# Eleven groups of seven block products per MLP in place of seven, with two of each group's weight sums by accumulating DMA

## The chip, the core and the metric

The kernel runs on one NeuronCore of a Trainium2 chip, in one launch, with all operands in HBM at the start and the result in HBM at the end. The metric is the device time of that launch in microseconds (us), the median of several runs. A core has five engines that matter here, each with an instruction queue that it works off in order: TensorE (PE: matmuls and, beside them, weight loads), VectorE (DVE), ScalarE (ACT), GpSimd (POOL), and SyncE (SP), which here only starts DMA transfers. Engines wait for one another, and for transfers, on semaphores.

## What is computed

A decoder trunk of two layers on 256 tokens of width 2048, in float32: an RG-LRU block, an MLP, a dilated attention block, a second MLP, and a final RMSNorm. The change touches the two MLPs alone:

```python
def _mlp(h, w1, w2):
    u = jnp.einsum('bsd,df->bsf', h, w1)
    u = jnp.square(jax.nn.relu(u))
    return jnp.einsum('bsf,fd->bsd', u, w2)

x = x + _mlp(_rmsnorm(x, mlp_norm[i]), mlp_w1[i], mlp_w2[i])
```

Here `w1` is 2048 x 8192 and `w2` is 8192 x 2048.

## The kernel before

**Two-part numbers.** A float32 product is made of three matmuls. Each operand is cut into a high part (float32r) and a low rest: ScalarE copies the high part (line 108, `whi`), VectorE subtracts it from the original (line 112, `wlo`), and TensorE adds high x high, high x low and low x high in PSUM.

**Units.** Weights come in units of 128 x 2048 floats (1 MB). For each, SP starts a load, ScalarE makes the high cut, VectorE the low cut, and TensorE uses both. There are three `raw` buffers for loads, three for high cuts and three for low cuts. The functions `before_unit` and `behind_unit` write out the program's order: the load of unit i + 5 is issued ahead of unit i's matmuls, the low cut of unit i + 2 too, and the high cut of unit i + 3 just behind them. So a high cut waits until TensorE has left the unit three earlier. Callbacks (`after`) put the small work on results behind a unit or one unit later.

**An MLP in periods.** The hidden width of 8192 is handled in 8 periods of 1024. In period p TensorE multiplies the squared activations of that part by their rows of `w2`, and between those units it makes the activations of the next period, in 8 units called "w" (`plan_first`, 48 matmuls of 256 columns each; `u_done` and `u_low`, lines 487 to 501, square, cut and store them). The output has four chunks of 512 columns, kept in SBUF as `xc`. In the plain way (`plan_plain`) a chunk of a period takes two units of 24 matmuls of 512 columns, marked "s" in the order.

**Groups.** `plan_group` takes two chunks together and computes the 2 x 2 x 2 block products (two halves of the tokens, two halves of the period's rows, two chunks) with seven products in place of eight, in the manner of Winograd's form of Strassen's method. Each product has 12 matmuls of 512 columns and is a unit of its own with its own pair of cuts. Four of them use the loaded blocks b11, b21, b12, b22 (in `raw`, `q21`, `q12` and `q22`), and three use sums of them. Line 570 makes four sums of whole units on VectorE: qT = b11 - q12 ahead of t1 and qT + q22 ahead of t2 (the signs lie in how they are written), then q12 with q22 ahead of t3 and q21 with qT ahead of t4. The tiles `q21`, `q12`, `q22` and `qT` have one buffer each. The products add up in three PSUM banks, and `take` (line 574) adds these to `xc`.

On the other side sums of token blocks are needed: `sums_of_tokens` (lines 503 to 517) makes them with five VectorE instructions and one of ScalarE, once per quarter of a period's rows and for all groups of the period. It holds them back while a product of the running period still reads the last ones; `busy` says so and is cleared at product t3 ("s3").

**The order.** `ORDER` lists a period's units by hand: the seven products, 8 "w" and 4 "s", 19 in all. Periods 0 to 6 have a group, the last has only plain units and no "w".

Of the kernel before, what the change touches and what calls it, by code (L numbers as in the profile page):

```python
# [13 lines left out]
OP = mybir.AluOpType  # L14
# [13 lines left out]
NCH = D // 512  # L28
# [16 lines left out]
SOFT = (5, 3, 3, 3, 3)  # L45
LOOK_LO = 2
LOOK_HI = 3
GROUPS = range(7)
ORDER = ("b11", "w", "b21", "s", "w", "t1", "w", "t2", "b22", "w", "s", "w", "t3", "w", "s", "w", "t4", "w", "s")


@with_exitstack
def trunk(ctx: ExitStack, tc: tile.TileContext, a: dict, out: bass.AP):
    nc = tc.nc
# [10 lines left out]
    def unit(ap, width=UW):  # L65
        units.append({"ap": ap, "width": width})
        return len(units) - 1
# [74 lines left out]
    def item(u, fn):  # L142
        items.append((u, fn))
# [23 lines left out]
    def after(n, fn, *args):  # L167
        later.setdefault(now[0] + n, []).append((fn, args))
# [82 lines left out]
    def stand_w(ps, u, ks, w_at, first, last):  # L251
        hi, lo = split[u]
        for j, k in enumerate(ks):
            x = xT(k)
            s = slice((w_at + j) * 128, (w_at + j + 1) * 128)
            mm(ps, hi[:, s], x[:, 0:256], first and j == 0, False)
            mm(ps, hi[:, s], x[:, 256:512], False, False)
            mm(ps, lo[:, s], x[:, 0:256], False, last and j == len(ks) - 1)
# [12 lines left out]
    def acc_tile():  # L271
        return psum.tile([P, 512], F32, name="acc", bufs=4)
# [12 lines left out]
    def add_x(n, acc):  # L285
        for t in range(NT):
            nc.vector.tensor_add(xc[n][:, t, :], xc[n][:, t, :], acc[t])
# [19 lines left out]
    def new_aT(j):  # L307
        t = (perm if j < 16 else lru).tile([P, 512], F32R, name=f"aT{j}")
        state["aT", j] = t
        return t  # L310
# [176 lines left out]
    def u_done(p, j, ps):  # L487
        h, k = divmod(j, 4)
        if h == 0:
            squares[p, k] = lru.tile([P, 2, S], F32, name="uu", bufs=4)  # L490
        uu = squares[p, k][:, h, :]
        nc.vector.scalar_tensor_tensor(uu, ps[:, :S], 0.0, state["rstdB"], op0=OP.max, op1=OP.mult)
        nc.scalar.activation(uu, uu, AF.Square)
        t = new_aT(8 * (p % 2) + j)
        nc.scalar.activation(t[:, 0:256], uu, AF.Copy)
        after(1, u_low, t, uu)
        if h == 1 and p in GROUPS:
            after(1, waiting.append, (p, k))

    def u_low(t, uu):  # L500
# [29 lines left out]
    def plan_mlp(w1, w2, done):  # L530
        def plan_first(p, j):
            u = unit(w1[8 * p + j])

            def run():
                accs["u", p, j] = acc_tile() if p == 0 else psum.tile([P, 512], F32, name="g", bufs=2)
                stand_w(accs["u", p, j][:, :S], u, range(KD), 0, True, True)
                after(0, u_done, p, j, accs.pop(("u", p, j)))
            item(u, run)

        def plan_start():  # L540
            us = [unit(w1[j]) for j in (0, 4)]
            for at, ks in enumerate((range(0, 12), range(12, 16))):
                for u, j in zip(us, (0, 4)):
                    def run(u=u, j=j, ks=ks, at=at):
                        if at == 0:
                            accs["u", 0, j] = acc_tile()
                        stand_w(accs["u", 0, j][:, :S], u, ks, ks[0], at == 0, at == 1)
                        if at == 1:
                            after(1 if j == 0 else 0, u_done, 0, j, accs.pop(("u", 0, j)))
                    item(u, run)  # L550

        def plan_plain(p, n, h, last_part):
            u = unit(w2[((p // 2) * 4 + n) * 4 + (p % 2) * 2 + h])
            out_item(("m", n), u, aT, range(8 * (p % 2) + 4 * h, 8 * (p % 2) + 4 * h + 4), h == 0, h == 1,
                     done(n) if last_part else (lambda acc, n=n: add_x(n, acc)))

        def plan_group(p, n0):


            q, bank = {}, {}  # L560

            def fetch(name, h, n, tag):
                q[name] = (wts.tile([P, UW], F32, name="raw", bufs=RAW_BUFS) if tag == "raw"
                           else lru.tile([P, UW], F32, name=tag))
                nc.sync.dma_start(q[name], w2[((p // 2) * 4 + n0 + n) * 4 + (p % 2) * 2 + h])

            def add(to, a, b):
                if to not in q:
                    q[to] = lru.tile([P, UW], F32, name=to)
                nc.vector.tensor_add(q[to], q[a], q[b])  # L570

            def take(n, t, b, sign):
                x = xc[n0 + n][:, t, :]
                (nc.vector.tensor_add if sign > 0 else nc.vector.tensor_sub)(x, x, bank[b])

            def product(loads, sums, source, what, b, first, takes):
                def load_all():
                    for l in loads:
                        fetch(*l)

                def make_all():
                    for m in sums:
                        add(*m)
                u = form(load_all, make_all, lambda: q[source])

                def run():
                    if first:
                        bank[b] = acc_tile() if b != "A" else psum.tile([P, 512], F32, name="tr", bufs=2)
                    hi, lo = split[u]
                    get = standing(p, what)  # L590
                    for k in range(4):
                        xh, xl = get(k)
                        s = slice(k * 512, (k + 1) * 512)
                        mm(bank[b], xh, hi[:, s], first and k == 0, False)
                        mm(bank[b], xh, lo[:, s], False, False)
                        mm(bank[b], xl, hi[:, s], False, k == 3)
                    for t in takes:
                        after(0 if what == "a22" else 1, take, *t)
                    if what == "s3":
                        busy[0] = None  # L600
                    if what == "a11":
                        busy[0] = p
                item(u, run)

            return {
                "b11": lambda: product([("b11", 0, 0, "raw")], [], "b11", "a11", "A", True, [(0, 0, "A", 1)]),
                "b21": lambda: product([("q21", 1, 0, "q21")], [], "q21", "a12", "B", True, [(0, 0, "B", 1)]),
                "t1": lambda: product([("q12", 0, 1, "q12")], [("qT", "b11", "q12")], "qT", "s0", "C", True,
                                      [(1, 1, "C", -1)]),
                "t2": lambda: product([("q22", 1, 1, "q22")], [("qT", "qT", "q22")], "qT", "s1", "A", False,  # L610
                                      [(1, 0, "A", -1)]),
                "b22": lambda: product([], [], "q22", "s2", "C", False, [(1, 0, "C", -1)]),
                "t3": lambda: product([], [("q12", "q12", "q22")], "q12", "s3", "A", False, [(1, 1, "A", -1)]),
                "t4": lambda: product([], [("q21", "q21", "qT")], "q21", "a22", "A", False, [(0, 1, "A", 1)]),
            }

        plan_start()
        for j in (1, 5, 2, 6, 3, 7):
            plan_first(0, j)
        for p in range(8):  # L620
            if p == 7 and done is final_done:
                item(None, load_g)
            if p < 7:
                nxt = iter([(p + 1, j) for j in (0, 4, 1, 5, 2, 6, 3, 7)])
            plain = [(n, h) for n in range(2 if p in GROUPS else 0, NCH) for h in range(2)]
            g = plan_group(p, 0) if p in GROUPS else {}
            for what in (ORDER if p in GROUPS else ("s", "w") * 8):
                if what == "w":
                    if p < 7:
                        plan_first(*next(nxt))  # L630
                elif what != "s":
                    g[what]()
                elif p == 7 and plain[0][0] == NCH - 1 and done is final_done:
                    final_items([unit(w2[(12 + n) * 4 + 2 + h]) for n, h in plain])
                    break
                else:
                    plan_plain(p, *plain.pop(0), p == 7)
# [190 lines left out]
    for n in range(NCH):  # L828
        xg[n] = new_xg(n)
        rs = [wts.tile([P, UW], F32, name="raw", bufs=RAW_BUFS) for _ in range(3)] if n == 0 else rs  # L830
        for h in range(2 if n == 0 else 1):
            w = 2 if n == 0 else 4
            nc.sync.dma_start(xg[n][:, h * w:(h + 1) * w, :], a["xT"][:, 4 * n + h * w:4 * n + (h + 1) * w, :])
            for i in range(3):
                if n or i == 0:
                    s = slice(n * 512 + h * w * 128, n * 512 + (h + 1) * w * 128)
                elif h:
                    s = slice(0, 512)
# [5 lines left out]
        for h in range(2 if n == 0 else 1):  # L844
            w = 2 if n == 0 else 4
# [31 lines left out]
    for n in range(NCH):  # L877
        s = slice(n * 512, (n + 1) * 512)
# [127 lines left out]
```

## Time and profile before

| | us |
|---|---|
| median of 3 runs | 2173.51 (2171.34 to 2175.61) |
| the profiled execution | 2173.91 |
| its span, first to last instruction | 2172.1 |
| TensorE busy | 2144.1 |
| VectorE busy | 1600.6 |
| ScalarE busy | 1167.5 |
| one period of an MLP, from the first product of one to that of the next | 86.30 |

The span is what the profiler sees between the first and the last instruction; the time has 1.8 us around it. A view of the profile shows instructions with their start, their duration in us, the engine, the line, what is written and read, and in square brackets how long the engine had been idle before and which instruction ended that wait. Matmuls overlap one another, so the pace of TensorE is the distance from one start to the next and not a matmul's duration.

### The profile page before, as it was taken

How to read it: one execution, taken by the hardware profiler on the slowest of the kernel's cores; microseconds unless marked ns; L12 is line 12 of the kernel's file. 1: busy time of each engine (PE TensorE's matmuls, PEld its weight loads, DVE VectorE, ACT ScalarE, POOL GpSimd, SP SyncE). 2: the span in 40 equal slices, each digit the busy share in tenths (PEclk: the TensorE clock that was granted, in tenths of full speed). 3: DMA queues.
4: the chain of work that ended last, by engine and by line, in shares of the span. 5: the costliest groups of instructions: out<-in, count | busy, mean ns of one | idle time of the engine just before them, and what ended most of it. 6: DMA issues, size and time to landing. Idle time of an engine off the chain costs nothing.

```text
span 2172.1 us, 32089 instructions
## 1 busy us (share of the span) xinstructions
PE 2144.1 (99%) x13602; PEld 1940.1 (89%) x13602; DVE 1600.6 (74%) x1748; ACT 1167.5 (54%) x1261; POOL 78.9 (4%) x42
## 2 busy tenths in 40 slices
PE   7999999999999999999999999999999999999997
PEld 7999988999999999999888888889999999999996
DVE  8898954688887888787555555556888878878875
ACT  5777755554555554455545544456455455554543
POOL 2221100000000000000000000000000000000002
PEclk9999999999999999999999999999999999999999
DMA  6565555556455455554554454455554563645543
GB/s 231 204 208 194 197 199 185 183 197 230 148 221 213 156 216 192 194 213 175 176 193 158 171 175 174 157 191 190 198 214 166 204 231 137 232 178 194 210 176 134
DMA packets 61712, 413.56 MB, mean 190 GB/s; under 512 B 6784, under 2 KB 7168, under 8 KB 13440
## 3 DMA queue, kind: packets, MB, share of 16 engines
q1 hardware_dynamic: 61568, 411.51, 52.1%
q8 instruction: 106, 1.74, 0.3%
q14 instruction: 38, 0.31, 0.0%
HBM read 409.39 MB, written 2.10 MB: 189 GB/s over the span
## 4 chain that ended last, share of the span: by engine, by line
PE 83%; DVE 10%; ACT 4%; issue 1%; POOL 0%; DMA 0%; SPq 0%; DVEq 0%; ACTq 0%
PE acc L171 53%; PE g L171 24%; DVE wlo L112 6%; PE tr L171 4%; ACT whi L108 2%; DVE q L570 1%; ACT sT L187 1%; DVE sT L188 0%; PE tr L211 0%; DVE aT L501 0%; DVE sw L512 0%; PE tr L670 0%; PE g L678 0%; DVE xT L849 0%; DVE sw L514 0%
## 5 line engine op out<-in xcount | busy, mean ns | idle before, releaser
L108 ACT ACTIVATE whi<-raw 128x2048 fp32r<-128x2048 f32 (+2 forms) x348 | 646.8, 1860 | 562.2 <-PE acc L171 336.5
L112 DVE TENSOR_TENSOR wlo<-raw,whi 128x2048 fp32r<-128x2048 f32 (+2 forms) x348 | 779.9, 2245 | 214.9 <-ACT whi L108 214.7
L171 PE MATMUL g<-xT,whi 128*128 128x256 f32 x3616 | 642.4, 281 | 0.0
L171 PE MATMUL acc<-whi,aT 128*128 128x512 f32 x1840 | 580.5, 390 | 0.0
L171 PEld LDWEIGHTS g<-xT,whi 128*128 128x128 f32 x3616 | 559.1, 188 | 8.7
L171 PE MATMUL g<-xT,wlo 128*128 128x256 f32 x1808 | 508.5, 281 | 2.2 <-DVE wlo L112 2.2
L171 PEld LDWEIGHTS acc<-whi,aT 128*128 128x128 f32 x1840 | 345.4, 188 | 69.6
L171 PE MATMUL acc<-wlo,aT 128*128 128x512 f32 x920 | 358.3, 389 | 0.0
L171 PEld LDWEIGHTS g<-xT,wlo 128*128 128x128 f32 x1808 | 346.2, 191 | 4.6 <-DVE wlo L112 4.6
L171 PE MATMUL acc<-xT,whi 128*128 128x256 f32 x1760 | 309.7, 281 | 6.5 <-ACT whi L108 6.1
L171 PEld LDWEIGHTS acc<-xT,whi 128*128 128x128 f32 x1760 | 270.7, 191 | 7.5 <-ACT whi L108 6.3
L171 PE MATMUL acc<-xT,wlo 128*128 128x256 f32 x880 | 247.2, 281 | 8.3 <-DVE wlo L112 8.1
L171 PE MATMUL acc<-whi,xT 128*128 128x512 f32 x768 | 245.9, 396 | 0.0
L171 PEld LDWEIGHTS acc<-wlo,aT 128*128 128x128 f32 x920 | 172.8, 188 | 33.4
L108 ACT ACTIVATE whi<-q 128x2048 fp32r<-128x2048 f32 x56 | 107.2, 1914 | 176.4 <-DVE q L570 137.8
L171 PEld LDWEIGHTS acc<-xT,wlo 128*128 128x128 f32 x880 | 168.0, 191 | 9.6 <-DVE wlo L112 9.4
L171 PEld LDWEIGHTS acc<-whi,xT 128*128 128x128 f32 x768 | 144.3, 188 | 30.6
L171 PE MATMUL acc<-wlo,xT 128*128 128x512 f32 x384 | 150.4, 392 | 0.0
L112 DVE TENSOR_TENSOR wlo<-q,whi 128x2048 fp32r<-128x2048 f32 x56 | 128.2, 2289 | 19.2 <-ACT whi L108 19.2
L108 ACT ACTIVATE whi<-qT 128x2048 fp32r<-128x2048 f32 x28 | 53.7, 1918 | 132.8 <-DVE qT L570 132.8
L112 DVE TENSOR_TENSOR wlo<-qT,whi 128x2048 fp32r<-128x2048 f32 x28 | 64.2, 2292 | 47.9 <-ACT whi L108 47.9
L171 PEld LDWEIGHTS acc<-wlo,xT 128*128 128x128 f32 x384 | 72.2, 188 | 15.1
(175 smaller groups left out, 1940.3 us busy)
## 6 DMA issues: line engine op xcount, KB each, us to landing
raw<-in_w SPq DMA_DIRECT2D x214, 1024.0 KB, 4.8
raw<-in_w_qkv SPq DMA_DIRECT2D x48, 1024.0 KB, 4.8
q<-in_w SPq DMA_DIRECT2D x42, 1024.0 KB, 6.9
raw<-in_w_in SPq DMA_DIRECT2D x35, 1024.0 KB, 4.8
raw<-in_w_out SPq DMA_DIRECT2D x20, 1024.0 KB, 4.8
raw<-in_w_o SPq DMA_DIRECT2D x16, 1024.0 KB, 4.8
raw<-in_w_g SPq DMA_DIRECT2D x10, 512.0 KB, 3.4
raw<-in_w_in SPq DMA_DIRECT2D x11, 256.0 KB, 5.7
```

Of the source, the lines that this page charges most:

```text
L108: nc.scalar.activation(split[i][0][:, s], r, AF.Copy)
L112: nc.vector.tensor_sub(split[i][1][:, s], r, split[i][0][:, s].bitcast(F32))
L171: nc.tensor.matmul(o, l, r, start=start, stop=stop, skip_group_check=True)
L187: nc.scalar.activation(hi_out, src, AF.Copy)
L570: nc.vector.tensor_add(q[to], q[a], q[b])
```

## The change

`GROUPS` becomes a number of groups for each period, 2, 1, 2, 1, 2, 1, 2, 0, and `ORDER` has a list for each number. A period of two covers all four chunks by groups: 14 products and 8 "w", no plain unit. Its second group's b11 stands ahead of the first group's t4. Periods of one keep their order. The two sums ahead of t3 and t4 are no longer VectorE instructions. An accumulating DMA, started by GpSimd, adds q22 to q12 and qT to q21 in SBUF; both are issued where t2's sum is made. `busy` is cleared at t3 of a period's last group. All lines behind the table move down by 7 to 11.

```diff
-GROUPS = range(7)
-ORDER = ("b11", "w", "b21", "s", "w", "t1", "w", "t2", "b22", "w", "s", "w", "t3", "w", "s", "w", "t4", "w", "s")
+GROUPS = (2, 1, 2, 1, 2, 1, 2, 0)
+ORDER = {
+    0: ("s", "w") * 8,
+    1: ("b11 0", "w", "b21 0", "s", "w", "t1 0", "w", "t2 0", "b22 0", "w", "s", "w", "t3 0", "w", "s", "w", "t4 0", "w", "s"),
+    2: ("b11 0", "w", "b21 0", "t1 0", "w", "t2 0", "b22 0", "w", "t3 0", "b11 1", "t4 0", "w",
+        "b21 1", "t1 1", "w", "t2 1", "b22 1", "w", "t3 1", "w", "t4 1", "w"),
+}
...
-        if h == 1 and p in GROUPS:
+        if h == 1 and GROUPS[p]:
             after(1, waiting.append, (p, k))
...
             def add(to, a, b):
+                if to == a != "qT":
+                    nc.gpsimd.dma_start(q[to], q[b], accum_op=OP.add)
+                    return
...
-                    if what == "s3":
+                    if what == "s3" and last_group:
                         busy[0] = None
...
-                "t2": lambda: product([("q22", 1, 1, "q22")], [("qT", "qT", "q22")], "qT", "s1", "A", False,
+                "t2": lambda: product([("q22", 1, 1, "q22")], [("qT", "qT", "q22"), ("q12", "q12", "q22"),
+                                                  ("q21", "q21", "qT")], "qT", "s1", "A", False,
...
-                "t3": lambda: product([], [("q12", "q12", "q22")], "q12", "s3", "A", False, [(1, 1, "A", -1)]),
-                "t4": lambda: product([], [("q21", "q21", "qT")], "q21", "a22", "A", False, [(0, 1, "A", 1)]),
+                "t3": lambda: product([], [], "q12", "s3", "A", False, [(1, 1, "A", -1)]),
+                "t4": lambda: product([], [], "q21", "a22", "A", False, [(0, 1, "A", 1)]),
...
-            plain = [(n, h) for n in range(2 if p in GROUPS else 0, NCH) for h in range(2)]
+            plain = [(n, h) for n in range(2 * GROUPS[p], NCH) for h in range(2)]
```

The first place where the order differs is VectorE's queue, from the low cut of b21 to that of t2's sum, in a period with one group of before. A row is the line, the operation, and what it writes from what; numbers tell the buffers apart.

```order
L112 TENSOR_TENSOR wlo_6082<-q21_5960,whi_6067 128x2048
L112 TENSOR_TENSOR wlo_6101<-raw_5980,whi_6097 128x2048
L574 TENSOR_TENSOR xc0_68<-xc0_68,tr_6084 128x512
L492 SCALAR_TENSOR_TENSOR uu_6155<-g_6103,rstdB_4114 128x256
L112 TENSOR_TENSOR wlo_6162<-raw_6039,whi_6152 128x2048
L570 TENSOR_TENSOR qT_6177<-raw_5859,q12_6080 128x2048
L501 TENSOR_TENSOR aT8_6158<-uu_6155,aT8_6158 128x256
L112 TENSOR_TENSOR wlo_6182<-qT_6177,whi_6179 128x2048
L574 TENSOR_TENSOR xc0_68<-xc0_68,acc_6164 128x512
L112 TENSOR_TENSOR wlo_6215<-raw_6099,whi_6210 128x2048
L570 TENSOR_TENSOR qT_6177<-qT_6177,q22_6160 128x2048
```

Two other low cuts (a plain unit and a "w") stand between the cut of b21 and the sum for t1. Now VectorE's queue in a period of two of the changed kernel, from the first group's t4 (the cut of `q21_5967`) to the second group's t1 and t2.

```order
L119 TENSOR_TENSOR wlo_6367<-q21_5967,whi_6357 128x2048
L508 TENSOR_TENSOR aT9_6363<-uu_6360,aT9_6363 128x256
L119 TENSOR_TENSOR wlo_6386<-raw_6285,whi_6381 128x2048
L584 TENSOR_TENSOR xc1_69<-xc1_69,tr_6091 128x512
L119 TENSOR_TENSOR wlo_6406<-q21_6304,whi_6401 128x2048
L580 TENSOR_TENSOR qT_6420<-raw_6208,q12_6365 128x2048
L584 TENSOR_TENSOR xc2_70<-xc2_70,tr_6388 128x512
L584 TENSOR_TENSOR xc0_68<-xc0_68,tr_6091 128x512
L119 TENSOR_TENSOR wlo_6426<-qT_6420,whi_6422 128x2048
L499 SCALAR_TENSOR_TENSOR uu_6360<-g_6428,rstdB_4114 128x256
L119 TENSOR_TENSOR wlo_6485<-raw_6384,whi_6477 128x2048
L580 TENSOR_TENSOR qT_6420<-qT_6420,q22_6404 128x2048
```

The sum for t1 now stands directly behind the low cut of b21, and that cut (`q21_6304`) only two cuts behind the last one that reads the old contents of the same buffer.

The second place is the SP queue, with what each load waits for in brackets: here of before, from b11 of a period (`raw_5859`) to its q22.

```order
L565 DMA raw_5859<-in_w2_0 128x2048 [waits DMAHW4_49,DVE_49,Activation_49]
L87 DMA raw_5900<-in_w1_0 128x2048 [waits DMAHW5_49,DVE_49,Activation_49]
L565 DMA q21_5960<-in_w2_0 128x2048
L87 DMA raw_5980<-in_w2_0 128x2048 [waits DMAHW6_49,DVE_49]
L87 DMA raw_6039<-in_w1_0 128x2048 [waits DMAHW0_49,DVE_49]
L565 DMA q12_6080<-in_w2_0 128x2048
L87 DMA raw_6099<-in_w1_0 128x2048 [waits DMAHW2_49,DVE_49]
L565 DMA q22_6160<-in_w2_0 128x2048
```

And the changed kernel's loads of the second group of a period of two, from its b11 (`raw_6208`) to its q22; DMASW is an accumulating DMA.

```order
L572 DMA raw_6208<-in_w2_0 128x2048 [waits DMAHW7_49,DVE_49]
L94 DMA raw_6285<-in_w1_0 128x2048 [waits DMAHW3_49,DVE_49]
L572 DMA q21_6304<-in_w2_0 128x2048 [waits DMASW7_49,DVE_49]
L572 DMA q12_6365<-in_w2_0 128x2048 [waits DMAHW1_49,DMASW6_49]
L94 DMA raw_6384<-in_w1_0 128x2048 [waits DMAHW5_49,DMAHW2_49]
L572 DMA q22_6404<-in_w2_0 128x2048 [waits DMAHW4_49]
```

The load of the group's q21 had nothing to wait for before; it now waits for the accumulating DMA into that buffer and for VectorE, and the three loads behind it stand in line.

More of the change, by code (lines that the diff above doesn't have):

```diff
@@ L555, in plan_plain, with plan_group @@
                      done(n) if last_part else (lambda acc, n=n: add_x(n, acc)))
-        def plan_group(p, n0):
+        def plan_group(p, n0, last_group):
             q, bank = {}, {}
@@ L624, in plan_mlp @@
                 nxt = iter([(p + 1, j) for j in (0, 4, 1, 5, 2, 6, 3, 7)])
-            plain = [(n, h) for n in range(2 if p in GROUPS else 0, NCH) for h in range(2)]
-            g = plan_group(p, 0) if p in GROUPS else {}
-            for what in (ORDER if p in GROUPS else ("s", "w") * 8):
+            plain = [(n, h) for n in range(2 * GROUPS[p], NCH) for h in range(2)]
+            g = [plan_group(p, 2 * n, n == GROUPS[p] - 1) for n in range(GROUPS[p])]
+            for what in ORDER[GROUPS[p]]:
                 if what == "w":
@@ L631, in plan_mlp @@
                 elif what != "s":
-                    g[what]()
+                    g[int(what[-1])][what[:-2]]()
                 elif p == 7 and plain[0][0] == NCH - 1 and done is final_done:
```

## The prediction

> **What bounds the kernel now.** I read the page first, for the engines' shares.
>
> ```profile
> span 2172.1 us, 32089 instructions
> PE 2144.1 (99%) x13602; PEld 1940.1 (89%) x13602; DVE 1600.6 (74%) x1748; ACT 1167.5 (54%) x1261; POOL 78.9 (4%) x42
> ```
>
> TensorE is busy throughout, but a share over the whole span says nothing about one stage. So next come the windows of single periods in the first MLP, cut where a period's first product starts (columns: us, then PE, PEld, DVE, ACT, POOL busy, granted clock, DMA share, GB/s).
>
> ```profile
> 688.80:775.10 86.30, 86.12 (x566) 78.90 (x565) 70.77 (x72) 44.14 (x39) 0.00 (x0) 1.00 0.53 197
> 775.10:861.40 86.30, 86.12 (x566) 78.89 (x565) 70.50 (x71) 44.07 (x39) 0.00 (x0) 1.00 0.52 195
> ```
>
> Every period takes 86.30 us, TensorE fills it, and VectorE is busy for 70.6, which leaves it 15.7. The chain of waits in that window gives the price of each kind of unit on TensorE: a "w" (48 matmuls), a product (12), a plain half chunk (24).
>
> ```profile
> 705.48 5.65 PE g L171 x48
> 711.13 2.72 PE acc L171 x12
> 730.60 5.44 PE acc L171 x24
> ```
>
> 8 x 5.65 + 7 x 2.72 + 4 x 5.44 = 86.0: a period is TensorE's work without gaps, so fewer matmuls make it shorter only if the weights keep arriving. The last view is VectorE's timeline at a period's start, with TensorE's rows there.
>
> ```profile
> 774.61 1.37 DVE L287 TENSOR_TENSOR xc<-xc,acc 128x512 f32<-128x512 f32 x2 [0.31 <-PE acc L171]
> 775.89 0.29 DVE L511 TENSOR_TENSOR sw<-uu 128x128 f32<-128x128 f32 x1
> ...
> 777.75 0.69 DVE L188 TENSOR_TENSOR sT<-sw,sT 128x512 fp32r<-128x512 f32 x1 [0.72 <-ACT sT L187]
> 778.36 2.29 DVE L112 TENSOR_TENSOR wlo<-q,whi 128x2048 fp32r<-128x2048 f32 x1
> 780.57 2.28 DVE L112 TENSOR_TENSOR wlo<-raw,whi 128x2048 fp32r<-128x2048 f32 x1
> 782.77 0.68 DVE L574 TENSOR_TENSOR xc<-xc,tr 128x512 f32<-128x512 f32 x1
> 783.66 0.42 DVE L492 SCALAR_TENSOR_TENSOR uu<-g,rstdB 128x256 f32<-128x256 f32 x1 [0.21 <-PE g L171]
> 785.49 2.29 DVE L112 TENSOR_TENSOR wlo<-raw,whi 128x2048 fp32r<-128x2048 f32 x1 [1.41 <-ACT whi L108]
> 787.70 2.29 DVE L570 TENSOR_TENSOR qT<-raw,q 128x2048 f32<-128x2048 f32 x1
> 789.90 0.42 DVE L501 TENSOR_TENSOR aT<-uu,aT 128x256 fp32r<-128x256 f32 x1
> 792.03 2.29 DVE L112 TENSOR_TENSOR wlo<-qT,whi 128x2048 fp32r<-128x2048 f32 x1 [1.71 <-ACT whi L108]
> ```
>
> ```profile
> 775.09 0.39 PE L171 MATMUL tr<-whi,aT 128*128 128x512 f32 x1
> ...
> 783.46 0.39 PE L171 MATMUL acc<-whi,aT 128*128 128x512 f32 x1
> ...
> 797.27 0.39 PE L171 MATMUL acc<-whi,sT 128*128 128x512 f32 x1
> 797.50 0.39 PE L171 MATMUL acc<-wlo,sT 128*128 128x512 f32 x1
> ```
>
> Three prices follow. A full-width VectorE pass takes 2.29 us and the next starts 2.20 after it. A weight sum delays the low cut of its own result by 4.33 (787.70 to 792.03), since ScalarE's high cut lies between and VectorE waits for it in order. Before the first low cut of a period VectorE must finish the last token sum: it starts it 3.27 after the period (778.36 against 775.09). And there is slack: t1's low half is ready at 794.32, and TensorE asks for it at 797.50, so 3.2 us are left.
>
> **The change: matmuls.** Each of the 8 added groups replaces 4 x 5.44 by 7 x 2.72: -2.72 us, -21.8 in all. It holds only if TensorE never waits, and the period of two is where that is in doubt. I number its units from 0: b11 0, w 1, b21 2, t1 3, w 4, t2 5, b22 6, w 7, t3 8, b11' 9, t4 10, w 11, b21' 12, t1' 13, w 14, t2' 15, b22' 16, w 17, t3' 18, w 19, t4' 20, w 21; T is the time from its start at which TensorE could begin a unit. The high cut of unit u can begin only when unit u-3 has left TensorE (three buffers); it did so 0.08 us after a w ended:
>
> ```profile
> 783.54 1.92 ACT L108 ACTIVATE whi<-raw 128x2048 fp32r<-128x2048 f32 x1 [3.62 <-PE g L171]
> 785.37 0.40 ACT L493 ACTIVATE uu<-uu 128x256 f32<-128x256 f32 x1
> ```
>
> and the low cut followed at 785.49, 1.95 after the high one began.
>
> **VectorE's first half (T0 to T8).** With the plain unit gone between b21 and t1, in VectorE's order: low cut of b21 at 3.27, sum for t1 at 5.47, t1's low cut at 9.80, ready at 12.09. TensorE wants it at 11.09 + 0.23 = 11.32: wait 0.77. Then an update of xc (0.60) and uu (0.33; each its duration less the 0.09 by which passes overlap), unit 4's low cut, ready at 15.23 against 14.81: 0.42. The second sum starts at 15.14, t2's low cut at 19.47, ready at 21.76 against 20.88: 0.88. Units 6 and 7 the same way: 0.08 and 0.42. Sum 2.57; T8 moves from 30.55 to 33.12.
>
> **The load of b21' (T8 to T13).** The SP queue issues in order, and the q21 buffer is read by b21 and again by t4. Its two rows:
>
> ```profile
> 699.19 2.29 DVE L112 TENSOR_TENSOR wlo<-raw,whi 128x2048 fp32r<-128x2048 f32 x1 [1.38 <-ACT whi L108]
> ...
> 701.51 2.53 SPq L87 DMA_DIRECT2D raw<-in_w x2
> ```
>
> ```profile
> DMA to landing us min/median/max: 4.7/6.9/8.8
> ```
>
> A load waiting for a low cut issues 0.03 after it (701.51 against 701.48), and a load of q lands 4.7 us later at best. Unit 12's load now waits for unit 10's low cut, and unit 10's high cut for T8. In a row from T8: 0.08, high cut 1.95, low cut 2.29, issue 0.03, landing 4.7: 9.05. Then b21's high cut 1.95, its low cut 2.20, the sum for t1' behind it in VectorE's order and t1's cuts 4.33, low cut 2.29: 19.82. TensorE wants it at three products, a w, b21' and 0.23 after T8: 8.16 + 5.65 + 2.72 + 0.23 = 16.76. Wait 3.06. Queued behind that load on SP are q12', w 14 and q22'; they land by T8 + 18 at 2.9 us apiece (1 MB at about 360 GB/s, an estimate: 190 GB/s at a queue share of 52.1%), in time for their cuts.
>
> ```profile
> q1 hardware_dynamic: 61568, 411.51, 52.1%
> HBM read 409.39 MB, written 2.10 MB: 189 GB/s over the span
> ```
>
> I take the minimum, 4.7, as SP was blocked before and the queue is then empty; by the median, 6.9, the wait would be 5.3 and the sum below 8 x 2.2 = 18 more. [...]
>
> **The second half.** Counting from the start of t1's low cut, the second sum comes at 4.73, t2's low cut is ready at 11.35 against 10.66 (0.69), units 16 and 17 wait 0.08 and 0.42. The token sums at the end (2.47 each, 775.89 to 778.36) pile up in the last four units and delay the next period's w by 0.79; not where the last period follows, which has no token sums. Sum 1.98.
>
> **Two sums per group by DMA.** They free VectorE of 2 x 2.20, already left out above, and on Pool they queue before nothing (its busy time in the windows is 0.00); in periods of one TensorE did not wait before, so nothing comes of it there. The trace has no accumulating DMA. From below it takes 4.7, a load's best. From above 17.6: twice the slowest load, 8.8, as two tensors are read. The first can begin when t1's sum has read q12, at 7.76, the second when t2's sum ends, at 17.43; the second must land by t4's high cut at 33.20. It has 15.8 us, or 12.7 each if the two go one behind the other. I take values nearer the load: no cost. [...]
>
> **The sum.** Per period of two: -2.72 + 2.57 + 3.06 + 1.98 = +4.89; eight of them +39.1; less 0.79 in each of the two layers' last: +37.5. On the profiled execution's own 2173.9 (span 2172.1 and 1.8 around it; the runs' median is 2173.5) that is 2211 us.
>
> **Rivals.** *TensorE alone decides (0.10).* VectorE's work in a period of two is 70.6 + 3 more full passes (3 more cuts; 4 sums as before) x 2.20 + 3 more updates of xc x 0.60: 79.0 of 83.6 us; if the buffers smooth this and t1' does not wait, the time is 2173.9 - 21.8 = 2152. The place is t1' (unit 13), and it decides where all waits of a period of two stay under 2.72. Against it: the 9.05 to landing and the 4.33 are both in rows, and make 3.06 alone.
> *Only the load of b21' costs (0.12).* VectorE's lateness is all of 0.4 to 0.9 us pieces, which small errors could remove: 8 x (3.06 - 2.72) = +2.7, 2176.6.
> *The accumulates land late (0.13).* At 17.6 each in a row the second lands at 43.0, 9.8 late, and the load of b21' with it: 8 x 9.8 more, 2290; it decides above 12.7 each. [...]
>
> **The numbers.** My forecast has 0.65, at 2211. The low end takes in the second rival, 2176; the high end accumulates of 14.8 us each (2.1 over 12.7, twice, in eight periods: +34), 2245. Outside lie 0.10 below and some 0.05 above. About 0.2% (4.3 us) is what a measurement can tell from no change: faster 0.10, same 0.12, slower 0.78.
>
> **What would show it.** Right: windows of about 91 us for periods of two and 86.3 for the others; TensorE waiting some 3 us on the low cut of qT at the second group's t1, behind an SP queue that waits for the low cut of q21; the accumulates landing within 12 us. Wrong: 83.6 us for periods of two, or the high cut of q21 or q12 waiting for the software DMA.

## The result, and the profile after

The changed kernel takes 2224.03 us (median of 4 runs, 2223.12 to 2225.34), the kernel before 2172.66 on the same chip (4 runs, 2171.34 to 2175.61): a ratio of 1.0233, with a 95% interval of 1.0221 to 1.0246. The forecast was 2211. The direction held, and the loss was about 14 us larger than the sum. Two of the forecast's mechanisms are in the trace as it worked them out, but the costliest wait is one that it did not have, and this one hides the load's wait that it did have: that the sum came near is in part luck.

The page of the changed kernel, its busy times and the chain that ended last:

```profile
span 2223.5 us, 32196 instructions
...
PE 2144.4 (96%) x13506; PEld 1925.2 (87%) x13506; DVE 1641.8 (74%) x1784; ACT 1218.0 (55%) x1285; POOL 117.1 (5%) x86
...
PE 72%; DVE 15%; ACT 7%; issue 3%; DMA 2%; POOL 0%; SPq 0%; DVEq 0%; ACTq 0%
```

There are 96 matmuls fewer, yet TensorE is busy for as long, and idle for 4% of the span in place of 1%. VectorE holds 15% of the chain. Neither line says where; the windows of one period of two and the period of one behind it do (columns as in the prediction):

```profile
608.69:702.15 93.46, 87.01 (x554) 77.78 (x552) 77.05 (x76) 49.46 (x40) 3.44 (x4) 0.98 0.66 206
702.15:788.17 86.02, 86.02 (x566) 79.02 (x565) 68.12 (x70) 45.38 (x41) 1.72 (x2) 1.00 0.70 242
```

14 products and 8 "w" need 83.3 us (14 x 2.72 + 8 x 5.65) and took 93.46. The forecast was 91.2 (86.30 + 4.89). The period of one, 86.02, is 0.28 shorter than before, where the forecast had no change.

**The first half came as worked out.** VectorE's rows at the start of that period:

```profile
611.97 2.28 DVE L119 TENSOR_TENSOR wlo<-q,whi 128x2048 fp32r<-128x2048 f32 x1
614.17 2.28 DVE L580 TENSOR_TENSOR qT<-raw,q 128x2048 f32<-128x2048 f32 x1
618.50 2.29 DVE L119 TENSOR_TENSOR wlo<-qT,whi 128x2048 fp32r<-128x2048 f32 x1 [2.04 <-ACT whi L115]
...
623.84 2.28 DVE L580 TENSOR_TENSOR qT<-qT,q 128x2048 f32<-128x2048 f32 x1
...
628.16 2.29 DVE L119 TENSOR_TENSOR wlo<-qT,whi 128x2048 fp32r<-128x2048 f32 x1 [1.71 <-ACT whi L115]
```

From the period's start at 608.69 the forecast had the low cut of b21 at 3.27, the sums at 5.47 and 15.14 and the low cuts of qT at 9.80 and 19.47; the rows give 3.28, 5.48, 15.15, 9.81 and 19.47. TensorE's waits in the same period, in order:

```profile
620.84 0.50 PE L178 MATMUL acc<-wlo,sT 128*128 128x512 f32 x1 [0.67 <-DVE wlo L119]
630.51 0.50 PE L178 MATMUL tr<-wlo,sT 128*128 128x512 f32 x1 [0.61 <-DVE wlo L119]
634.00 0.47 PE L178 MATMUL acc<-whi,sT 128*128 128x512 f32 x1 [0.71 <-DVE xc L584]
...
647.71 0.39 PE L178 MATMUL tr<-whi,aT 128*128 128x512 f32 x1
650.40 0.76 PE L178 MATMUL tr<-whi,aT 128*128 128x512 f32 x1 [2.31 <-DVE xc L584]
650.96 0.63 PE L178 MATMUL tr<-wlo,aT 128*128 128x512 f32 x1
651.39 1.05 PE L178 MATMUL tr<-whi,aT 128*128 128x512 f32 x2
652.24 0.63 PE L178 MATMUL tr<-wlo,aT 128*128 128x512 f32 x1
...
675.11 0.47 PE L178 MATMUL acc<-whi,sT 128*128 128x512 f32 x1 [0.58 <-DVE xc L584]
...
693.66 0.47 PE L178 MATMUL tr<-whi,aT 128*128 128x512 f32 x1 [1.51 <-DVE xc L584]
```

The first two are the low halves of t1 and t2. Each costs the bracket and 0.16 to 0.18 more until the pace of 0.23 a matmul is back: 0.83 and 0.79, forecast 0.77 and 0.88. The third, b22, waits 0.87, and not for a cut: its releaser is line 584, a take. The fourth, at 650.40, is the costliest and in no term of the forecast: t4 starts 2.46 us late, again for a take. After it single matmuls stand 0.43 apart in place of 0.23; the granted clock from 650.40 to 653.50 is 0.50. The last two rows are b22 and t4 of the second group, 0.73 and 1.68 late, for takes again.

**What t4 waits for.** VectorE from t4's low cut on, and then the SP queue, from the load of b21':

```profile
644.53 2.29 DVE L119 TENSOR_TENSOR wlo<-q,whi 128x2048 fp32r<-128x2048 f32 x1 [1.41 <-ACT whi L115]
...
647.37 2.29 DVE L119 TENSOR_TENSOR wlo<-raw,whi 128x2048 fp32r<-128x2048 f32 x1 [0.21 <-ACT whi L115]
649.58 0.68 DVE L584 TENSOR_TENSOR xc<-xc,tr 128x512 f32<-128x512 f32 x1
653.67 2.29 DVE L119 TENSOR_TENSOR wlo<-q,whi 128x2048 fp32r<-128x2048 f32 x1 [3.42 <-ACT whi L115]
655.88 2.28 DVE L580 TENSOR_TENSOR qT<-raw,q 128x2048 f32<-128x2048 f32 x1
...
660.21 2.29 DVE L119 TENSOR_TENSOR wlo<-qT,whi 128x2048 fp32r<-128x2048 f32 x1 [0.85 <-ACT whi L115]
```

```profile
646.85 0.80 SPq L572 DMA_DIRECT2D q<-in_w  x2
```

The row at 649.58 is the take of t3. t3 and t4 add up in the same PSUM bank ("A" in the code), so t4 may begin only when VectorE has read t3's result out. The take is held back by one unit and stands behind the low cut of a "w" (647.37). With plain units and "w" between t3 and t4, as in a period of one, that costs nothing (TensorE is busy for all of the 86.02 above). In the period of two only b11' is between them.

Then the load of b21'. It was issued at 646.85, 0.03 after t4's low cut (644.53 + 2.29), as worked out. t4's high cut began at 642.58 (the profile's ScalarE row is below), 0.08 after T8 by the forecast's count, so t1's low cut should have been ready at 642.58 - 0.08 + 19.82 = 662.32; it was ready at 662.50.

```profile
642.58 1.92 ACT L115 ACTIVATE whi<-q 128x2048 fp32r<-128x2048 f32 x1 [3.62 <-PE g L178]
```

```profile
663.23 0.39 PE L178 MATMUL acc<-whi,sT 128*128 128x512 f32 x1
663.45 0.39 PE L178 MATMUL acc<-wlo,sT 128*128 128x512 f32 x1
```

But TensorE reached t1' only at 663.23, because t4 had held it up, and asked for the low half at 663.45. The 3.06 of the load was there and found nobody waiting.

**The accumulating DMAs came in time.** Their issues, from GpSimd, beside a plain load on SP (KB each, then median us to landing), and the landing of those that read qT, the second of each group:

```profile
raw<-in_w SPq DMA_DIRECT2D x190, 1024.0 KB, 5.1
...
q<-q POOLq DMA_DIRECT2D x22, 1024.0 KB, 11.6
q<-qT POOLq DMA_DIRECT2D x22, 1024.0 KB, 10.4
```

```profile
DMA to landing us min/median/max: 7.7/10.4/13.0
```

The DMA that reads qT starts last; even its slowest, 13.0, is within the 15.8 that the forecast gave it. All 44 together landed in 7.7 to 13.2 us. In the period shown 15.0 to 18.0 lie between the start of one's issue and the high cut that reads its result, and no high cut of the whole run waited for one.

### The profile page after: what moved, and what is told of

Its sections match the earlier page's. It is cut to its first block, busy times and chain, and to the rows that moved or that the text cites. A ratio compares the mean times of both kernels' runs of the same rounds, so it can differ in the third digit from the quotient of the medians.

```text
span 2223.5 us, 32196 instructions
## 1 busy us (share of the span) xinstructions
PE 2144.4 (96%) x13506; PEld 1925.2 (87%) x13506; DVE 1641.8 (74%) x1784; ACT 1218.0 (55%) x1285; POOL 117.1 (5%) x86
## 4 chain that ended last, share of the span: by engine, by line
PE 72%; DVE 15%; ACT 7%; issue 3%; DMA 2%; POOL 0%; SPq 0%; DVEq 0%; ACTq 0%
PE acc L178 46%; PE g L178 20%; DVE wlo L119 8%; ACT whi L115 6%; PE tr L178 4%; DVE qT L580 3%; DMA q<-in_w 2%; DVE xc L584 1%; DMA xg<-in_xT 0%; PE tr L218 0%; ACT sT L194 0%; PE tr L681 0%; PE g L689 0%; DMA raw<-in_w_in 0%; DVE xT L860 0%
## 5 line engine op out<-in xcount | busy, mean ns | idle before, releaser
L115 ACT ACTIVATE whi<-raw 128x2048 fp32r<-128x2048 f32 (+2 forms) x324 | 600.9, 1857 | 499.7 <-PE acc L178 328.9
L119 DVE TENSOR_TENSOR wlo<-raw,whi 128x2048 fp32r<-128x2048 f32 (+2 forms) x324 | 724.4, 2240 | 172.7 <-ACT whi L115 172.3
L178 PE MATMUL acc<-whi,aT 128*128 128x512 f32 x1392 | 440.3, 391 | 0.0
L178 PEld LDWEIGHTS acc<-whi,aT 128*128 128x128 f32 x1392 | 261.3, 188 | 52.7
L178 PE MATMUL acc<-wlo,aT 128*128 128x512 f32 x696 | 271.1, 390 | 0.0
L115 ACT ACTIVATE whi<-q 128x2048 fp32r<-128x2048 f32 x88 | 168.2, 1911 | 155.2 <-PE g L178 98.5
L119 DVE TENSOR_TENSOR wlo<-q,whi 128x2048 fp32r<-128x2048 f32 x88 | 201.4, 2289 | 62.6 <-ACT whi L115 62.6
L178 PEld LDWEIGHTS acc<-wlo,aT 128*128 128x128 f32 x696 | 130.7, 188 | 25.3
L119 DVE TENSOR_TENSOR wlo<-qT,whi 128x2048 fp32r<-128x2048 f32 x44 | 100.8, 2292 | 66.8 <-ACT whi L115 66.8
L178 PE MATMUL tr<-whi,aT 128*128 128x512 f32 x352 | 121.0, 405 | 27.5 <-DVE xc L584 27.5
## 6 DMA issues: line engine op xcount, KB each, us to landing
q<-q POOLq DMA_DIRECT2D x22, 1024.0 KB, 11.6
q<-qT POOLq DMA_DIRECT2D x22, 1024.0 KB, 10.4
```

Of the source, the lines that this page charges most:

```text
L115: nc.scalar.activation(split[i][0][:, s], r, AF.Copy)
L119: nc.vector.tensor_sub(split[i][1][:, s], r, split[i][0][:, s].bitcast(F32))
L178: nc.tensor.matmul(o, l, r, start=start, stop=stop, skip_group_check=True)
```

## The experiments

My theory after the result: in a period of two, four sequences cost time, and they hide one another: the take of t3 in front of t4, the load of b21' in front of t1', the chain of sum and cuts in front of t1 and t2, and the takes in front of b22 and t4'. The rivals were a slower chip under the accumulating DMAs, VectorE's total work, and the load alone.

**1. The DMA sums without the groups.**

```diff
-GROUPS = (2, 1, 2, 1, 2, 1, 2, 0)
+GROUPS = (1, 1, 1, 1, 1, 1, 1, 0)
```

Expected: 

> One group in each of periods 0 to 6 as before, with the two sums of each group by accumulating DMA: the second part of the change alone. Order theory (TensorE waits in periods of two because of the order of cuts, takes and loads there): no change, 2173 within 4 us, TensorE without waits in every period, since it had none before and VectorE only gets lighter. Rival, the accumulating DMAs cost by themselves (traffic, late landing): the 51.4 us of the change spread over 22 accumulates-pairs, 2.3 us each, so 14 groups make about 33 us, 2206.

Measured 2169.77 against 2173.51: 0.9983 (0.9973 to 0.9992). Two neighbouring periods of it, and a row of the kernel before that comes in each of periods 0 to 5 of both MLPs:

```profile
601.58:687.60 86.02, 86.02 (x565) 79.01 (x564) 66.50 (x69) 44.39 (x39) 1.70 (x2) 1.00 0.65 220
687.60:773.62 86.02, 86.02 (x565) 79.01 (x564) 66.51 (x69) 44.40 (x39) 1.71 (x2) 1.00 0.65 220
```

```profile
678.00 0.39 PE L171 MATMUL g<-xT,wlo 128*128 128x256 f32 x1 [0.18 <-DVE wlo L112]
```

The accumulating DMAs do no harm; they gain 0.28 in each of these 12 periods, 12 x 0.28 = 3.4 us, since the kernel before had that one small wait at a "w" for a low cut, and the two sums less on VectorE remove it.

**2. The groups without the DMA sums**, the sums of t3 and t4 back on VectorE:

```diff
-                if to == a != "qT":
-                    nc.gpsimd.dma_start(q[to], q[b], accum_op=OP.add)
-                    return
```

Expected: 

> Eleven groups in the new order, but all four sums of a group on VectorE at their old places: the first part of the change alone. Order theory: VectorE, which is late in the period of two already, gets 4 more passes of 2.20 us there and up to 1.7 us of waiting for the high cut behind each, 9 to 14 us in 8 periods: 2295 to 2335. Rival, the accumulates are the cost: without them the time falls below 2200.

Measured 2329.22 against 2173.51: 1.0712 (1.0694 to 1.0730). Its waits of TensorE for a take, us in total, times and the longest:

```profile
PE tr L178 <- DVE xc L581: 106.6, 32, 6.2
```

So the two halves of the change are not alike: without the DMAs the groups cost three times as much, and they do so through the same wait (27.5 us in total and 2.3 the longest in the changed kernel), since each VectorE pass ahead of a take, 2.28 us for a sum there, delays it.

**3. The take of t3 at once**, ahead of the low cut of the "w":

```diff
-                        after(0 if what == "a22" else 1, take, *t)
+                        after(0 if what in ("a22", "s3") else 1, take, *t)
```

Expected: 

> The changed kernel, with the result of t3 added to xc directly behind t3 instead of one unit later, so that t4 need not wait for its bank. Theory: the bank wait at the first group's t4 (2.46 us, with up to 1.7 us of slower matmuls behind it) hides the load wait of 3.06 us predicted for the second group's t1. Then t4 and the second t4 wait no more, t1 of the second group waits about 3.1 us in each of the 8 periods, and the time is 2205 to 2215. Rival, the bank wait alone counts and the load is in time: no wait at the second t1, 8 times 5 us less, about 2184.

Measured 2218.93 against 2173.51: 1.0211 (1.0196 to 1.0226). Every wait at t4 is gone. TensorE in the same period of two, at t1':

```profile
659.18 0.50 PE L178 MATMUL acc<-whi,sT 128*128 128x512 f32 x1 [0.92 <-ACT whi L115]
661.51 0.50 PE L178 MATMUL acc<-wlo,sT 128*128 128x512 f32 x1 [1.82 <-DVE wlo L119]
```

Here is the forecast's load term: 1.08 and 2.10 with the pauses behind the brackets, 3.18 together, against 3.06. One wait was taken away and the next stood in its place, so only 0.2% came of it. That is 4 us above the range expected: part of t1' runs at half pace here (its matmuls stand 0.43 apart in place of 0.23 from 663.11 to 665.25), and the first "w" of the next period waits some 0.8, which t4' hides in the changed kernel.

**4. The same without the load of b21'.** The second group does not fetch q21 and uses what is in the buffer, on top of experiment 3:

```diff
+                if name == "q21" and n0:
+                    q[name] = kept[p]
+                    return
```

Expected: 

> The changed kernel with the result of t3 added at once, and without the load of the second group's b21: 8 loads are left out, and the second group computes with the old contents of that buffer. Theory: the load behind t4's low cut is the whole of the 3.2 us wait at the second t1 (1.1 for the high cut, 2.1 for the low cut), so that wait goes and with it the slower matmuls behind it: 2219 less 8 times 3.2, about 2190. Rival, VectorE's order behind t4 makes the wait: less than 8 us gained, 2211 or more.

Measured 2189.43 against 2170.63: 1.0086 (1.0069 to 1.0103). The wait at t1' is gone, and a period of two is 3.4 us shorter for it (1.25% of 2172, by eight). So the load did set that place. The 0.8 at the next period's first "w" stands here as in experiment 3; the forecast had it at 0.79.

**5. The order spread out**: one unit "w" between t3 and t4, b11' behind t4, so that both the take and the load have time:

```diff
-    2: (..., "t3 0", "b11 1", "t4 0", "w", "b21 1", ..., "t3 1", "w", "t4 1", "w"),
+    2: (..., "t3 0", "w", "t4 0", "b11 1", "w", "b21 1", ..., "t3 1", "w", "t4 1"),
```

Expected: 

> The changed kernel with another order of the period of two: a w between t3 and t4 of the first group, t4 ahead of the second group's b11, a w behind that b11, and the last w between t3 and t4 of the second group. Theory: this gives the bank its take and the load of b21 some 6 us more, so both waits vanish; what stays is VectorE's lateness at t1, the w behind it, t2 and b22, 0.8 + 0.3 + 0.8 + 0.9 us in each half, 5.6 us a period: 89.2 us a period, about 2196. Rival, the accumulating DMAs are the cost: no gain, 2224.

Measured 2209.98 against 2173.51: 1.0171 (1.0156 to 1.0186), 14 us above what was expected. Both waits went, and t1, t2, t2' and both b22 waited 0.7 to 1.0 each, as expected. But in the six periods of two that a period of one follows t4' kept its 1.68, with a "w" between it and t3', and b21 of the next period now waited 0.97 for its low half. I had priced neither: 6 x 2.65 is 15.9 us.

**6. Spread out, and each sum one unit earlier:**

```diff
-        step("make", i + LOOK_HI, make)
+        step("make", i + LOOK_HI + 1, make)
...
-        step("make", i + 1 + LOOK_HI, make)
+        step("make", i + 2 + LOOK_HI, make)
```

Expected: 

> The spread order of the run before, and each weight sum issued one unit earlier, so that a low cut stands on VectorE between a sum and the low cut of its result. Theory: VectorE's 1.7 to 2.1 us of waiting for ScalarE's high cut behind each of four sums a period is what makes the low halves of t1, w, t2 and b22 late; filled, it leaves 2.5 to 4 us of waits a period instead of 7.3, about 2182. Rival, VectorE's volume (some 82 of 83.6 us) and not its order makes it late: 2205 or more.

Measured 2179.60 against 2170.63: 1.0040 (1.0025 to 1.0055), 1.3% below experiment 5. What is left of TensorE's waits between 600 and 2100 us, which leaves out the first period of two of the first MLP and the last of the second (us in total, times and the longest):

```profile
PE g L178 <- DVE wlo L119: 9.5, 14, 1.3
PE tr L178 <- DVE xc L584: 7.6, 5, 1.5
PE acc L178 <- DVE wlo L119: 4.0, 5, 0.8
```

**7. Earlier sums alone**, without the new order:

Expected: 

> The changed kernel in its own order, with each sum one unit earlier and nothing else. Theory: the lateness at t1, w, t2 and b22 of the first half (0.83 + 0.33 + 0.78 + 0.87 us) shrinks to one wait of about 0.9 at the w behind t1, 1.9 us less a period; the bank wait at t4 (2.46 us) and the second t4's (1.7) stay; one low cut now also stands ahead of the second t1's. 8 times 1.9 to 3 less: 2200 to 2209. Rival, the sums' place does not matter as long as the banks and the load wait: 2220 or more.

Measured 2260.94 against 2173.25: 1.0399 (1.0384 to 1.0415). I had the sign wrong. VectorE, and then TensorE at t4:

```profile
652.18 2.29 DVE L119 TENSOR_TENSOR wlo<-raw,whi 128x2048 fp32r<-128x2048 f32 x1 [0.21 <-ACT whi L115]
658.84 2.29 DVE L580 TENSOR_TENSOR qT<-raw,q 128x2048 f32<-128x2048 f32 x1 [4.36 <-DMA q<-in_w]
661.05 0.68 DVE L584 TENSOR_TENSOR xc<-xc,tr 128x512 f32<-128x512 f32 x1
```

```profile
661.88 0.77 PE L178 MATMUL tr<-whi,aT 128*128 128x512 f32 x1 [8.96 <-DVE xc L584]
```

The sum for t1' now stands ahead of the take of t3, and it needs q12', whose load is queued on SP behind the late one of b21'. VectorE stands still for 4.36 with the take behind it, and t4 waits 9.12. The same edit gains 1.3% in the spread order and loses 1.6% here: an edit of an order has no price of its own.

**8. All of it, and small work off VectorE**: experiment 6, the take of t3 at once, and the low cuts of the activations and of the token sums on GpSimd:

```diff
-        nc.vector.tensor_sub(t[:, 256:512], uu, t[:, 0:256].bitcast(F32))
+        nc.gpsimd.tensor_sub(t[:, 256:512], uu, t[:, 0:256].bitcast(F32))
...
-        hilo(t[:, 0:4], t[:, 4:8], w)
+        nc.scalar.activation(t[:, 0:4], w, AF.Copy)
+        nc.gpsimd.tensor_sub(t[:, 4:8], w, t[:, 0:4].bitcast(F32))
```

Expected: 

> Spread order, sums one unit earlier, the result of t3 added at once, and the low cuts of the activations and of the token sums on GpSimd (0.33 us eight times, and some 1.9 us four times a period, off VectorE). Theory: with VectorE some 10 us lighter, in order, and both late loads and banks out of the way, a period of two takes 83.6 to 84.5 us: 2153 to 2162, faster than both kernels. [...]

Measured 2164.34 against 2170.63: 0.9973 (0.9962 to 0.9984), the first version that is faster than the kernel before, and 2 us above the range expected. One wait is left in each group, 0.84 at the "w" behind t1. No run tells apart what the take at once and what GpSimd's share of the work gained.

**9. Experiment 8 without the earlier sums:**

Expected: 

> As the run before, but the sums at their old place, directly ahead of the cut of their result. Theory: the waits of 1.7 to 2.1 us behind the sums stay on VectorE's path, in both halves, and cost 2 to 4 us a period of two: 2170 to 2188. Rival, VectorE's volume alone counted: as fast as the run before.

Measured 2197.06 against 2170.63: 1.0123 (1.0108 to 1.0138), above what was expected: t1, t2 and b22 wait 0.81, 0.98 and 0.86 as before. VectorE is busy for 1587.3 us here and for 1640.6 in experiment 5, and these waits are the same in both; moved one unit earlier, the sums take all three away (experiment 8). So the row of dependent steps, sum, high cut, low cut, was their cause, and these 53 us of VectorE's work were not.

**10. b22 ahead of t2**, on top of experiment 8: q22 then has its own cuts first, and t2's sum comes a unit later against its product; the take of t1's bank ("s0") is done at once.

```diff
-    2: (..., "t1 0", "w", "t2 0", "b22 0", "w", "t3 0", ...),
+    2: (..., "t1 0", "w", "b22 0", "t2 0", "w", "t3 0", ...),
```

Expected: 

> The fastest version so far (spread order, early sums, results of t3 at once, low cuts of activations and token sums on GpSimd), with b22 ahead of t2 in every group and the result of t1 added at once, so that the sum for t2 stands behind the low cut of the w and not ahead of it. Theory: the last wait, 0.84 us at the w behind t1 in all 22 groups (18 us), goes, and all periods of two take 83.6 us: 2144 to 2150. Rival, the wait moves to b22 or t2: 2158 to 2166.

Measured 2155.80 (2152.21 to 2156.51) against 2173.25: 0.9913 (0.9898 to 0.9928). It beats both kernels, and is 6 us above the range expected. In a period of two and the period of one behind it TensorE's only wait is this:

```profile
701.58 0.39 PE L178 MATMUL g<-xT,wlo 128*128 128x256 f32 x1 [0.67 <-DVE wlo L119]
```

It comes at six places in the run. The sum closes: 8 x 2.72 saved by matmuls, 12 x 0.28 by the DMA sums, and 6 x 0.83 waited is 2173.25 - 21.8 - 3.4 + 5.0 = 2153.1, within the runs' range. VectorE's sum for t1 ahead of the late low cut took 3.38 in place of 2.28, beside a low cut on GpSimd; without these 1.10 the wait of 0.83 would by these rows be gone, which no run tests.

**11. The same with two groups in every period:**

```diff
-GROUPS = (2, 1, 2, 1, 2, 1, 2, 0)
+GROUPS = (2, 2, 2, 2, 2, 2, 2, 0)
```

Expected: 

> As the run before, with two groups in all of periods 0 to 6: 28 groups in place of 22. Theory: TensorE alone decides now, 6 times 2.72 us less than the run before, about 2130. Rival, VectorE has no light period left in which to catch up and is late in each: no better than the run before, 2146 or more.

Measured 2166.65 against 2173.25: 0.9970 (0.9958 to 0.9981), where I expected another gain. TensorE's waits of one of its periods:

```profile
614.42 0.50 PE L178 MATMUL acc<-wlo,sT 128*128 128x512 f32 x1 [1.51 <-DVE wlo L119]
617.72 0.38 PE L178 MATMUL g<-xT,wlo 128*128 128x256 f32 x1 [0.23 <-DVE wlo L119]
623.41 0.47 PE L178 MATMUL acc<-whi,sT 128*128 128x512 f32 x1 [0.19 <-DVE xc L585]
```

With the pauses behind them 1.67, 0.39 and 0.35, 2.4 us, which is nearly the 2.72 that the second group saves. My reading, which no run tests by itself: VectorE comes out of each period of two late, and without a lighter period of one behind it the lateness stands at t1 of the next; alternating periods buy the time to catch up. VectorE's rows ahead of that t1 show a rival:

```profile
602.60 3.38 DVE L581 TENSOR_TENSOR qT<-raw,q 128x2048 f32<-128x2048 f32 x1
...
611.02 0.29 DVE L518 TENSOR_TENSOR sw<-uu 128x128 f32<-128x128 f32 x1 [1.18 <-POOL sT L524]
```

The sum took 1.10 longer than 2.28 beside GpSimd's cuts, and VectorE then stood still for 1.18, since the tile of the token sums has one buffer and GpSimd was still cutting the last one. Together that is more than the wait of 1.67, so the work moved to GpSimd may be what makes t1 late here; a run with the cuts back on VectorE would tell.

## Why the prediction was right, and where it was short

**Matmuls.** -2.72 a period of two: right. Experiment 10, where nearly nothing waits, gets all of it.

**VectorE's first half, +2.57.** Right in each time of VectorE up to t2, to 0.01 us. The waits were 0.83 at t1, about 0.3 at the "w" behind it and 0.79 at t2; b22 waited 0.87 in place of 0.08, for a take, and the "w" behind it hardly at all. These are 2.82, and with small pauses t3 began at 33.80 (642.49 - 608.69) in place of 33.12.

**The load of b21', +3.06.** The mechanism was right in every link and the size too (3.18 in experiment 3, gone in experiment 4). But in the changed kernel it costs nothing or 0.6 to 0.7, as t4 delays TensorE by more ahead of it: the largest term of the forecast is not in the measured time.

**The step that failed** is in "The load of b21' (T8 to T13)": it lets TensorE run from T8 through t3, b11' and t4 in "three products". t4 could not begin. The step asked of each unit whether its cuts were ready, and never whether the PSUM bank that it adds to had been read out; a take was counted only as 0.60 us of VectorE's time. t4's wait of 2.46, and of 1.68 at t4', were the two largest single waits of a period. The order shown ahead of the prediction had the fact in it: the take of `tr_6091` stands behind the low cut of `raw_6285` there, with t4's products due ahead of it.

**The second half, +1.98.** t2' waited 0 to 0.56 (0.69 forecast), b22' 0.73 to 0.87, t4' 1.68 (not forecast), the next period's "w" nothing (0.79 forecast, hidden by t4').

**The sum.** The listed waits of the period shown are 0.83, 0.33, 0.79, 0.87, 2.46, 0.73 and 1.68, and t4's slow matmuls add 1.70 (6.88 from its due start to its end, less 2.46 and 2.72). That is 9.4; less 2.72 and less 0.28 in the period of one, a pair of periods should take 6.4 more than before. It took 179.48, and 172.60 before: 6.9, the rest in pauses under 0.25. The forecast had 4.89. Over eight pairs that is 8 x 2.0 = 16; in each layer's last period of two t4' did not wait, which takes off 2 x 1.68 where the forecast had taken off 2 x 0.79, and leaves the 14 us. Of the 9.4 only 1.95 hang on low cuts, which is what the forecast added up; 7.4 hang on takes (b22 and t4 of both groups, with the slow matmuls), which it had at nothing. The sum came near all the same, because t4's wait stands where the load's would have stood (experiment 3, without it, is only 5 us faster); that the two are of a like size was luck.

**DMA sums.** "Nothing comes of it" in periods of one was 0.28 too little in each but the last of an MLP. The row that shows the small wait was in the trace, and the window of 86.30 against 86.0 of listed work hinted at it.

**The rivals.** TensorE alone: refuted as the kernel stands, and right in what it says is to be had once the order allows it (experiment 10). Only the load: refuted, the 0.4 to 0.9 pieces were real. The accumulates land late: refuted, 7.7 to 13.2 us with 15.0 or more to spend. VectorE's total work as the cause, by experiment 9, is no explanation for the waits at t1 and t2; for periods of two in a row (experiment 11) it stays open, beside the delays that GpSimd's cuts bring.

**Left open.** Why the slow matmuls came behind t4's wait in 4 of 8 periods and not in the others. In those others t1' and t2' waited some 0.6 each instead, so a pair of periods took 179.30 and 179.46 us in either case (from the end of t4's wait to that of the next: 471.10, 650.40, 829.86).

## What to carry to other kernels

When a change cuts work on the busiest engine, write down for each of its units all that must be true before it starts: operands ready, their buffers free, and the accumulator it writes read out; the last was forgotten here. In a hand-written order waits hide one another, so a removed wait is worth only the distance to the next one, and the gain comes when the whole row of them has been moved. The matmuls saved here gave +2.3% in one order and -0.9% in another, which also had some small work moved to GpSimd.

## What the hardware showed that was not expected

**TensorE at half pace after a short wait.** Behind t4's wait of 2.46 us the matmuls came at 0.43 apart in place of 0.23, in 4 of 8 periods, and never behind t4' with 1.68. In each of the four the granted clock is 0.50 for 3.4 us, from t4's start on in one (650.40) and from 1.1 to 1.5 us later in the others; behind the t4 at 471.10, after the same wait, it is 1.00. What sets the half clock off, and why only in some periods, no run shows.

**An accumulating DMA of 1 MB within SBUF** takes 7.7 to 13.2 us to land, with medians of 10.4 and 11.6 twice a plain load's 5.1, and did not slow VectorE's passes: the low cut at 618.50, beside the one issued at 616.98, took 2.29, as such cuts did on average in the kernel before, and the 44 sums took 2.28 to 2.29.

**GpSimd's subtract beside VectorE's passes.** The sum for t1 in experiment 6, and in experiment 8 with the low cuts on GpSimd (us in total, mean ns):

```profile
L580 DVE TENSOR_TENSOR qT<-raw,q 128x2048 f32<-128x2048 f32 x22 | 50.2, 2284 | 0.3 <-DMA q<-in_w 0.3
```

```profile
L581 DVE TENSOR_TENSOR qT<-raw,q 128x2048 f32<-128x2048 f32 x22 | 66.1, 3004 | 0.4 <-DMA q<-in_w 0.3
```

It takes 0.7 us longer on average. One of them in experiment 8, from GpSimd's timeline and VectorE's:

```profile
595.84 2.09 POOL L508 TENSOR_TENSOR aT<-uu,aT 128x256 fp32r<-128x256 f32 x1 [6.28 <-ACT aT L502]
```

```profile
597.26 2.83 DVE L581 TENSOR_TENSOR qT<-raw,q 128x2048 f32<-128x2048 f32 x1
```

The two overlap for 0.67 us (597.26 to 597.93), and the sum, which began second, is 0.55 longer than 2.28: part of what was moved away from VectorE came back. VectorE's low cut before it (595.05 to 597.34), which began ahead of GpSimd's subtract and overlaps it for 1.50, took its usual 2.29. What the two contend for no run shows.
